# Softmax over 16,384 rows on one core: row tiles of 15 in place of tiles of up to 25

## The chip, the cores and the metric

The kernel runs on one core of a Trainium2 chip. The metric is the time of one execution on the device, in microseconds. The time before is the median of four executions, 160.37 us, with a lowest of 159.57 and a highest of 161.0. A separate execution was recorded by the hardware profiler; all rows of a profile in this document come from such single executions.

## The reference

The input is a float32 array of 16 x 1024 rows of 512 elements. Every row gets a softmax with temperature 2:

```python
x_scaled = x / 2.0
x_max = np.max(x_scaled, axis=-1, keepdims=True)
exp_x = np.exp(x_scaled - x_max)
return exp_x / np.sum(exp_x, axis=-1, keepdims=True)
```

The data is 33.55 MB in and 33.55 MB out, and there is no reuse between rows.

## The kernel before

**Tiles.** The 16,384 rows are 128 partitions x 128 rows. A tile of r rows takes 128 x r consecutive rows of the input and puts r of them on each partition, so that each partition's piece is one contiguous run of r x 2 KB, both in the input and on the chip. `TILES` (line 10) lists the tiles as (rows, place in the arena). There are 8 of them, called tile 0 to tile 7 here: 3, 5, 15, 25, 25, 25, 20 and 10 rows. The arena (`ARENA`, line 13) holds 98 rows, and everything is computed in place in it. The first six tiles fill it exactly; tiles 6 and 7 begin again at its start, over tiles that have been stored.

**Loads.** Each tile is loaded by one DMA. SP issues load 0 and ACT all others. Loads 0 and 1 are put ahead of the entry barrier (`early`, lines 152 to 154); load 1 is cut into three DMAs (`SPREAD`, line 114). Loads 2 to 5 follow at once (`loads`, lines 156 to 158). Loads 6 and 7 are the late ones (`LATE`, line 12): ACT waits until the stores of the tiles that they overwrite have landed (stores 0, 1, 2 for load 6, store 3 for load 7), and then issues them. `TURNS` (line 20) says where in ACT's program this happens: load 6 after the exponentials of row 72, load 7 after those of row 97.

**Exponentials.** ScalarE (ACT) takes exp(x / 2) of one row of all 128 partitions at a time, with the row's sum as a second output (line 276; line 200 for the first 3 rows). The maximum isn't subtracted; the sums are checked at the end, as told below. The rows go in chunks of `E` = 5, in the loop `exponentials` (lines 264 to 281). Before each chunk ACT takes one count of the semaphore `s_go`, which PE raises when a tile has landed (lines 189 and 190), so that PE does nothing but translate "tile landed" into "so many chunks may go" (and one small matmul at the end).

**Scaling.** VectorE (DVE) takes the reciprocals of the sums (line 165) and multiplies the rows by them (line 168). One pair of instructions serves a group of chunks of the same tile: up to 3 chunks (15 rows), or up to 2 (10 rows) for the late tiles (line 82). That makes 12 pairs.

**Stores.** SP issues one store per tile, in order, when the last group of the tile has been multiplied (`store`, lines 132 to 134, called in line 214). Last, SP waits until all stores have landed (lines 261 and 262).

**The check of the sums.** When all exponentials are done, GpSimd and VectorE count the sums that lie between 1 and 1e30, PE adds the counts over the partitions, and VectorE writes a flag (lines 175 to 186). If a sum lay outside, the loops in `rounds` would compute everything again with the maximum subtracted. With this input they run no round. VectorE, ACT and GpSimd wait there for the last store but one (`s_near`).

Of the kernel before, what the change touches and what calls it, by code (L numbers as in the profile page):

```python
# [6 lines left out]

TILES = [(3, 0), (5, 3), (15, 8), (25, 23), (25, 48), (25, 73), (20, 0), (10, 20)]  # L10

LATE = {6: (0, 1, 2), 7: (3,)}
ARENA = 98

HEAD = [3]
# [1 line left out]

SPREAD = 1

TURNS = {6: 73, 7: 98}  # L20

LO, HI = 1.0, 1.0e30
G = 64
# [3 lines left out]
def kernel(  # L27
# [16 lines left out]
    n_rows = N // P  # L44
    assert sum(r for r, _ in TILES) == n_rows

# [11 lines left out]
    tiles, base = [], 0  # L58
    for r, at in TILES:
        assert at == base % ARENA  # L60
# [11 lines left out]
    straight = sum(HEAD)  # L72
# [6 lines left out]

    pairs = []  # L80
    for k, t in enumerate(owner):
        most = 2 if t in LATE else 3
        if pairs and len(pairs[-1]) < most and owner[pairs[-1][0]] == t:
            pairs[-1].append(k)
        else:
            pairs.append([k])
    upto = [1 + max(j for j, ks in enumerate(pairs) if owner[ks[0]] == t) for t in range(len(tiles))]

    ld = [nc.alloc_semaphore(f"ld{t}") for t in range(len(tiles))]
    s_home = {t: nc.alloc_semaphore(f"s_home{t}") for t in LATE}  # L90
    s_near = nc.alloc_semaphore("s_near")
# [18 lines left out]
    def load(eng, t):  # L110
        r = tiles[t][1]
        parts = [(0, P, 0, r)]
        if t == SPREAD:
            parts = [(0, P, 0, r - 1), (0, 126, r - 1, r), (126, P, r - 1, r)]
        for p, q, lo, hi in parts:
            eng.dma_start(
                out=sb(t)[p:q, lo:hi], in_=dram(xf, t)[p:q, lo:hi]
            ).then_inc(ld[t], 16)

    stored_by = {u: s_home[t] for t, us in LATE.items() for u in us}  # L120
    for t, (_, r, at) in enumerate(tiles):
        over = {u for u, (_, ru, au) in enumerate(tiles[:t]) if at < au + ru and au < at + r}
        assert over <= {u for v, us in LATE.items() if v <= t for u in us}

    def landings(ts):
        return 16 * len(list(ts))
# [9 lines left out]
    def take(eng, sem, n):  # L136
        eng.wait_ge(sem, n).then_inc(sem, -n)  # L137
# [18 lines left out]
    def loads():  # L156
        for t in range(2, min(LATE)):
            load(nc.scalar, t)

    def program():  # L160
# [36 lines left out]
        for k, c in enumerate(HEAD):  # L197
# [4 lines left out]
                    accum_out=stats[:, b : b + 1],  # L202
                )
            ins.then_inc(s_exp, 1)
        done = straight
        for t, us in LATE.items():
            exponentials(done, TURNS[t])
            nc.scalar.wait_ge(s_home[t], landings(us))
            load(nc.scalar, t)
            done = TURNS[t]  # L210
        exponentials(done, n_rows)

        for t in range(len(tiles)):
            store(nc.sync, t)
# [49 lines left out]
    def exponentials(first, end):  # L264
        row = nc.scalar.alloc_register(f"row{first}")
        nc.scalar.reg_mov(row, first)
        with nc.scalar.While(lambda: nc.scalar.snap(row, min_val=first, max_val=end) < end):  # L267
            now = nc.scalar.snap(row, min_val=first, max_val=end - E)
            take(nc.scalar, s_go, 1)
            at = nc.s_assert_within(  # L270
                now % ARENA, 0, ARENA - E,
                skip_runtime_bounds_check_because="no chunk reaches over the arena's end",
            )
            for r in range(E):
                data = arena[:, r : ARENA - E + 1 + r][:, bass.ds(at, 1)]
                ins = nc.scalar.activation(  # L276
                    out=data, in_=data, func=Exp, scale=0.5,
                    accum_out=stats[:, r : n_rows - E + 1 + r][:, bass.ds(now, 1)],
                )
            ins.then_inc(s_exp, 1)  # L280
            nc.scalar.reg_add(row, row, E)
# [12 lines left out]
    nc.switch_body(here, parent=None, valid_engines=[i.engine for i in jumps])  # L294
    loads()
    program()


# [28 lines left out]
```

## Time and profile before

| what | value |
|---|---|
| median of 4 executions | 160.37 us (159.57 to 161.0) |
| the profiled execution, as a whole | 161.27 us |
| its span, from the first to the last event of the program | 159.9 us |
| exponentials, ACT line 276 | 125 x 615 ns, and 125 reads of the sum x 188 ns |
| multiply of 15 rows, DVE line 168 | 4 x 8157 ns |
| multiply of 10 rows | 6 x 5492 ns |
| multiply of 5 rows / of 3 rows | 2824 ns / 1758 ns, once each |
| loads of 6400 KB (25 rows), issue to landing | 52.4 us (median of 3) |
| load of 3840 KB (15 rows) | 15.0 us |
| stores of 6400 KB, issue to landing | 42.3 us (median of 3) |
| last load, 2560 KB: issued at 101.06 us | 31.2 us to landing |
| last store, 2560 KB: issued at 144.65 us | 15.2 us to landing |

The span is the time of the core from the program's first event to its last; what lies around it (1.37 us in this execution) isn't in the profile. "ACTq" and "SPq" in the rows are the instruction queues of ACT and SP: what an engine waits for there is a semaphore that such a queue instruction tests. "DMA" in the table of slices is the mean busy share of the core's 16 DMA engines in 40 equal slices of the span, in tenths. The TensorE clock granted was 1.0 throughout.

The stores are issued by SP at 10.0, 14.6, 35.7, 58.8, 79.6, 106.2, 128.3 and 144.65 us, and the late loads by ACT at 73.05 and 101.06 us.

### The profile page before, as it was taken

Reading aid. Unit: us, or ns where it says so; the run is one execution under the profiler, and the core shown is the slowest. Engines: PE = TensorE matmul, PEld = TensorE weight load, DVE = VectorE, ACT = ScalarE, POOL = GpSimd, SP = SyncE. Lnnn points to the kernel's source line nnn. Section 1 sums busy time; section 2 is a strip of 40 time slices with the busy share of each in tenths; the row PEclk is TensorE's granted clock in tenths of the full one; section 3 lists DMA queues with packets and bytes.
Section 4 is the critical chain, followed back from the end, with each engine's and each line's share of the span. In section 5 each row is a group of like instructions: output and inputs, shape, how many; then the busy total and the mean of one; then the engine's idle time right before and its main releaser. Section 6 shows DMA issues by size and latency. Waiting matters only on the chain. (4 is left out here: it accounts for less than half of the span.)

```text
span 159.9 us, 656 instructions
## 1 busy us (share of the span) xinstructions
PE 0.2 (0%) x2; PEld 0.1 (0%) x2; DVE 72.9 (46%) x27; ACT 80.5 (50%) x257; POOL 0.9 (1%) x6
## 2 busy tenths in 40 slices
PE   0000000000000000000000000000000000000000
PEld 0000000000000000000000000000000000000000
DVE  0056001990089960699900099950088900292000
ACT  0870598019996099990029995004996008700000
POOL 0000000000000000000000000000000000100000
DMA  7999999899989897999988999999898999898993
GB/s 266 389 484 416 484 459 436 374 402 492 479 320 446 361 520 343 448 456 538 410 384 379 537 405 407 471 394 466 374 487 364 471 492 423 387 451 369 410 441 154
DMA packets 2450, 67.12 MB, mean 420 GB/s; under 512 B 273, under 2 KB 273, under 8 KB 657
## 3 DMA queue, kind: packets, MB, share of 16 engines
q1 hardware_dynamic: 1296, 34.34, 50.1%
q10 hardware_dynamic: 1152, 32.77, 48.1%
q14 instruction: 2, 0.01, 0.0%
HBM read 33.55 MB, written 33.55 MB: 420 GB/s over the span
## 5 line engine op out<-in xcount | busy, mean ns | idle before, releaser
L276 ACT ACTIVATE arena<-arena x125 | 76.6, 615 | 53.6 <-ACTq L137 53.6
L168 DVE TENSOR_TENSOR arena<-arena,recip 128x5120 f32<-128x5120 f32 (+3 forms) x12 | 70.2, 5847 | 0.4
L165 DVE RECIPROCAL recip<-stats 128x10 f32<-128x10 f32 (+3 forms) x12 | 2.6, 220 | 71.6 <-ACT arena L276 63.6
L276 ACT ACTIVATION_READ_ACCUMULATOR arena<-arena x125 | 23.4, 188 | 0.0
L196 ACT ACT_TABLE_LOAD x1 | 1.3, 1283 | 4.6 <-issue 4.6
L200 ACT ACTIVATE arena<-arena 128x512 f32<-128x512 f32 x3 | 1.9, 618 | 0.2 <-ACTq L137 0.2
L175 POOL TENSOR_SCALAR inside<-stats 128x128 f32<-128x128 f32 x1 | 0.6, 633 | 136.2 <-ACT arena L276 136.2
L200 ACT ACTIVATION_READ_ACCUMULATOR arena<-arena 128x1 f32 x3 | 0.6, 185 | 0.0
L192 PE MATMUL total<-ones,count 128*1 128x1 f32 x2 | 0.2, 164 | 144.9 <-DVE inside L179 144.9
L179 DVE SCALAR_TENSOR_TENSOR inside<-inside,stats 128x128 f32<-128x128 f32 x1 | 0.3, 284 | 0.0
L183 DVE TENSOR_SCALAR flag<-total 1x1 int32<-1x1 f32 x1 | 0.1, 147 | 0.3 <-PE total L192 0.3
L192 PEld LDWEIGHTS total<-ones,count 128*1 128x1 f32 x2 | 0.1, 82 | 144.9 <-DVE inside L179 144.9
L174 POOL MEMSET ones<- 128x1 f32 x1 | 0.1, 98 | 2.2 <-POOLq L35 2.2
L311 POOL MEMSET const-bfloat16-1.0<- 128x1 bf16 x1 | 0.1, 101 | 0.0
L311 POOL MEMSET const-uint8-127<- 128x1 uint8 x1 | 0.1, 101 | 0.0
L311 POOL MEMSET const-float32-0.0<- 128x1 f32 x1 | 0.1, 98 | 0.2 <-issue 0.2
L311 POOL MEMSET const-float32-1.0<- 128x1 f32 x1 | 0.1, 98 | 0.0
L179 DVE DVE_READ_ACCUMULATOR inside<-inside,stats 128x1 f32 x1 | 0.1, 82 | 0.0
## 6 DMA issues: line engine op xcount, KB each, us to landing
arena<-in_x_dram ACTq DMA_DIRECT2D x3, 6400.0 KB, 52.4
out_dram<-arena SPq DMA_DIRECT2D x3, 6400.0 KB, 42.3
arena<-in_x_dram ACTq DMA_DIRECT2D x1, 5120.0 KB, 36.7
out_dram<-arena SPq DMA_DIRECT2D x1, 5120.0 KB, 25.6
arena<-in_x_dram ACTq DMA_DIRECT2D x1, 3840.0 KB, 15.0
out_dram<-arena SPq DMA_DIRECT2D x1, 3840.0 KB, 37.3
arena<-in_x_dram ACTq DMA_DIRECT2D x1, 2560.0 KB, 31.2
out_dram<-arena SPq DMA_DIRECT2D x1, 2560.0 KB, 15.2
```

Of the source, the lines that this page charges most:

```text
L165: nc.vector.reciprocal(out=recip[:, b : b + c], in_=stats[:, b : b + c])._wait_ge(s_exp, ks[-1] + 1).then_inc(s_rec, 1)
L168: nc.vector.tensor_mul(out=arena[:, a : a + c], in0=arena[:, a : a + c], in1=recip[:, b : b + c].unsqueeze(2).to_broadcast([P, c, D]),)._w ...
L174: nc.gpsimd.memset(ones[:, :], 1.0).then_inc(s_ones, 1)
L175: nc.gpsimd.tensor_scalar(out=inside[:, :], in0=stats[:, :], scalar1=LO, scalar2=HI, op0=Alu.max, op1=Alu.min,)._wait_ge(s_exp, len(sizes) ...
L179: nc.vector.scalar_tensor_tensor(out=inside[:, :], in0=inside[:, :], scalar=1.0, in1=stats[:, :], op0=Alu.mult, op1=Alu.is_equal, accum_ou ...
L183: nc.vector.tensor_scalar(out=flag[:, :], in0=total[:, :], scalar1=float(N), scalar2=float(n_rows // G), op0=Alu.is_ge, op1=Alu.mult,)._wa ...
L192: nc.tensor.matmul(total[:, :], lhsT=count[:, :], rhs=ones[:, :], start=True, stop=True)._wait_ge(s_cnt, 2).then_inc(s_tot, 1)
L196: nc.scalar.preload_act_table(Exp)
L200: ins = nc.scalar.activation(out=arena[:, b], in_=arena[:, b], func=Exp, scale=0.5, accum_out=stats[:, b : b + 1],)
L276: ins = nc.scalar.activation(out=data, in_=data, func=Exp, scale=0.5, accum_out=stats[:, r : n_rows - E + 1 + r][:, bass.ds(now, 1)],)
L311: nc = _bacc.Bacc("TRN2", target_bir_lowering=False, num_devices=1)
```

## The change

Tiles 3 to 7 become tiles 3 to 9, of 15 rows each. The places of tiles 0 to 2 stay. Six tiles of 15 rows follow the first two and end at row 98 of the arena, as before; the last two of 15 rows lie over its start, tile 8 over tiles 0, 1 and the larger part of tile 2, tile 9 over the rest of tile 2 and a part of tile 3. So loads 2 to 7 are issued at the start, and loads 8 and 9 are the late ones, with the waits that loads 6 and 7 had: stores 0, 1, 2 for load 8, store 3 for load 9.

ACT issues both late loads at one place, after the exponentials of row 82 (`TURN`), the end of tile 6. The loop of exponentials is entered twice instead of three times.

VectorE's groups are 3 chunks (15 rows) in all tiles but the last, where each chunk of 5 rows is a group of its own. With these tiles that makes 12 pairs again: 3, 5, seven times 15, and three times 5 rows.

The last store covers 15 rows instead of 10, and the last store but one (`s_near`) 15 rows instead of 20.

```diff
-TILES = [(3, 0), (5, 3), (15, 8), (25, 23), (25, 48), (25, 73), (20, 0), (10, 20)]
-
-LATE = {6: (0, 1, 2), 7: (3,)}
+TILES = [
+    (3, 0), (5, 3), (15, 8), (15, 23), (15, 38), (15, 53), (15, 68), (15, 83), (15, 0), (15, 15),
+]
+
+LATE = {8: (0, 1, 2), 9: (3,)}
...
-TURNS = {6: 73, 7: 98}
+TURN = 83
...
-        most = 2 if t in LATE else 3
+        most = 1 if t == len(tiles) - 1 else 3
...
-        done = straight
+        exponentials(straight, TURN)
         for t, us in LATE.items():
-            exponentials(done, TURNS[t])
             nc.scalar.wait_ge(s_home[t], landings(us))
             load(nc.scalar, t)
-            done = TURNS[t]
-        exponentials(done, n_rows)
+        exponentials(TURN, n_rows)
```

## The prediction

> **What bounds the kernel now.** I read the page's busy rows first, then its DMA rows, then SP's waits and the timeline of the end. In this first fence, the engines, the DMA share by slice, and the two queues (q10 carries ACT's loads, q1 SP's stores and the first load):
>
> ```profile
> span 159.9 us, 656 instructions
> PE 0.2 (0%) x2; PEld 0.1 (0%) x2; DVE 72.9 (46%) x27; ACT 80.5 (50%) x257; POOL 0.9 (1%) x6
> ...
> DMA  7999999899989897999988999999898999898993
> ...
> q1 hardware_dynamic: 1296, 34.34, 50.1%
> q10 hardware_dynamic: 1152, 32.77, 48.1%
> ...
> HBM read 33.55 MB, written 33.55 MB: 420 GB/s over the span
> ```
>
> No compute engine is busy for more than half of the span; the 16 DMA engines are busy for 98% of it. The packet records behind these rows say it more sharply: one packet is one partition's piece of a tile, every engine carries 8 packets of each full DMA, and at every whole microsecond from 2 to 157 at least 15 of the 16 engines have a packet under way. While both queues hold work an engine takes one packet of each in turn. The median packet takes 234 ns (3 rows, 6144 B), 385 (5 rows), 761 (10 rows), 1138 (15 rows), 1514 (20 rows), 1891 (25 rows), in either direction. So the time is a sum: 8 x (234 + 385 + 1138 + 3 x 1891 + 1514 + 761) = 8 x 9705 = 77.6 us for the loads of one engine, the same for its stores, 155.3 us together. Most engines end their last data packet at 157.5 us; the missing 2.2 us are the start (first packets at 1.0 to 1.8 us) and stretched packets. Two engines end late, at 159.0 and 159.5, and the slower one lands at 159.9: it sets the span.
>
> Next, who waits for whom (line waited for: us, times, longest), and the end of the timeline (start, duration, engine, line):
>
> ```profile
> ACT arena L276 <- ACTq L137: 53.6, 7, 11.9
> ```
> ```profile
> SPq L134 <- DVE arena L168: 139.6, 8, 26.2
> SPq L262 <- DMA out_dram<-arena: 14.9, 1, 14.9
> ```
> ```profile
> 138.89 0.21 DVE L165 RECIPROCAL recip<-stats 128x10 f32<-128x10 f32 x1 [10.65 <-ACT arena L276]
> ...
> 139.13 5.49 DVE L168 TENSOR_TENSOR arena<-arena,recip 128x5120 f32<-128x5120 f32 x1
> ...
> 144.65 0.33 SPq L134 DMA_DIRECT2D out_dram<-arena  x1
> ```
>
> ACT waits for loads, and SP for VectorE, but neither wait holds the end. The last store is issued at 144.65, while the store before it has packets on the engines until 151.7 on most (153.5 on the slowest): the issue came 7 to 9 us ahead of its turn. The last 14.9 us are only queued stores draining. Two questions decide the change: does it alter the sum of packets, and does a queue ever run dry.
>
> **The change, part by part.** *Packets.* After: 8 x (234 + 385 + 8 x 1138) = 8 x 9723 = 77.8 us each way, 155.6 together: +0.29 us. Two more loads and two more stores also write 4 more completions per engine, 9 ns each: +0.04. The start of a DMA on the engines is the unknown: three starts in the trace stretch the packets beside them by some 0.35, 0.15 and 0.3 us (at 6.4, 13.9 and 45.6 us), the other fifteen or so show nothing on all engines. Four more starts thus cost 0 to 1.4 us; I take 0.1. Sum: +0.4 us.
>
> A rule speaks against the change here. The Trainium skill, page "DMA: Bandwidth & Descriptors", section "Anatomy of one DMA", gives each DMA a fixed cost of some 2.0 us beside its bytes (fitted for DMAs that GpSimd issues). Four more DMAs would be +8 us, 168.4. The row against it: the third load's first packet starts at 16.78, while the second's last one is ending (16.94), with no gap. With a later DMA already queued the fixed part is hidden, so I use the rows; the rule is worth its 2 us only where a queue is empty.
>
> *Issue.* ACT issues six 15-row loads up front instead of four loads. The four took 0.36, 0.46, 0.48 and 0.50 us, so two more are about 1.1 us, and the first exponential goes from 6.03 to about 7.1, the first store from 10.0 to 11.1. Loads queued until beyond 80 us cover that; without them it would be 1.1 us. ACT's two late loads (0.34 each) now both stand at row 83, where ACT would be waiting anyway. SP's two more issues (0.33 each) fall in its 139.6 us of waiting.
>
> *VectorE.* 12 multiplies before and after. Before, 33.0 + 32.6 + 2.8 + 1.8 = 70.2 us; after, 1.76 + 2.82 + 7 x 8.16 + 3 x 2.82 = 70.2. Per 15-row tile 9.2 us of exponentials and 8.4 of VectorE lie inside a period of 8 x 2 x 1.138 = 18.2 us. Zero, hidden by DMA.
>
> *Turns.* I walk the two queues with these durations, in us on a typical engine. The first store's packets began 3.64 after its issue (13.64), so now at 14.7. Beside 15-row loads it takes 8 x (0.234 + 1.138) = 11.0, to 25.7, the second 8 x (0.385 + 1.138) = 12.2, to 37.9. Taking the 2.2 lost us as lost by then, the loads have done 37.9 - 2.2 - 5.0 = 30.7 of their 77.8. Thereafter the turns are equal, 18.2 for each tile: loads 4 to 9 end at 41.1, 59.3, 77.5, 95.7, 113.9, 132.1; stores 2 to 6 end at 56.1, 74.3, 92.5, 110.7, 128.9; then store 7 alone from 132.1 to 139.6, store 8 to 148.7, store 9 to 157.8.
>
> *Waits.* Load 8 is issued when tile 6 is through ACT: 77.5 + 0.6 + 9.3 = 87.4, up to 1.9 later for a lagging engine. It needs stores 0 to 2 (56), and load 9 needs store 3 (74): both long home. Behind these waits on ACT stand only the exponentials of tile 7, whose load ends at 95.7; so the wait on store 3 costs nothing unless it slips by more than 13 us, and load 8 enters its queue 6 to 8 us before load 7 has drained (before: 7.1 and 6.4 us). A store is issued 18.4 after its load has ended (0.6 landing and wait, 9.3 ACT, 0.3 + 8.16 VectorE): stores 3 to 8 come 5 to 15 us ahead of their turns.
>
> *The end.* After the last load's last packet: 0.33 to land and 0.34 to the first exponential (131.95, 132.28, 132.62 in the trace), then 15 rows to the last reciprocal 9.32 (17.93 to 27.25 in the trace, against 6.27 for 10 rows), then reciprocal and 5-row multiply 3.05 (against 5.73) and 0.03: 13.1 us, against 12.7. With 1.9 us for a lagging engine store 9 is issued at 132.1 + 1.9 + 13.1 = 147.1. Its turn is at 148.7 on a typical engine and 150.6 on the lagging one, which sets the end: 3.5 us ahead. How long does an issue take to its first packet? 1.02 on an idle queue (the first load), 2.15 on ACT's, 3.64 behind busy packets (the first store). So 0 is what I book, with -0 and +0.1 at the trace's ends for the lagging engine; the others may idle half a us and still end before it. Where 8.8 us of cover stood, 3.5 are left.
>
> Against the profiled execution: 159.9 + 0.4 = 160.3 of span. That execution as a whole took 161.27, 1.37 more than its span and 0.9 more than the median of 160.37, so I put the 0.4 on the median: **160.8 us**.
>
> **Rivals.** *The stores run dry at the end (slower).* The last load needs all 16 engines, and turns can slip: the first store landed at 29.63 on its slowest engine, 28.14 on the next, a turn lost. If the last load loses one turn on the slowest engine it ends 1.14 later, and that engine's stores are 1.14 further: the cover falls by 2.3 to 1.2 us, against 1.0 to 3.6 needed, so 0 to 2.4 us are lost; two turns lose 2.1 to 4.7. It decides from a cover under about 2 us, and gives 161.8 to 164. For it: this is the thinnest cover in the ledger. Against: any time in which loads run alone (a late first store, a gap before store 2) brings the last load forward and adds cover.
>
> *The lag goes (faster).* The two late engines lost their time in single stretched packets of 25 rows (0.92 us at 45.6; 0.40, 0.30, 0.31 and 0.62 between 114 and 121). If that hangs on the big packets or on unequal turns, the span falls by 1.6 (third-latest engine) to 2.05: 160.8 - 1.6 = 159.2 to 158.7. Against: the other 25-row packets ran at 1891.
>
> *Each DMA pays its fixed cost:* 168.4, against the rows above.
>
> *The change does nothing that can be measured:* this is the likeliest case itself.
>
> **How the numbers follow.** Sum as worked out: 0.63, 159.6 to 161.8 (the four runs of before spread over 1.4 us). Dry at the end: 0.18. Lag goes: 0.16. Fixed cost or a thing unseen: 0.03. About 1%, that is 158.8 and 162.0, is what a measurement of this kernel can tell from no change. Faster by more needs the whole lag: 0.11. Slower by more: most of the dry case, the unseen one, and four costly starts: 0.20. Within: 0.69. The range takes the milder half of both rivals: 158.9 to 162.6.
>
> **What would show it.** Right: DMA slices as full as before, packets of 1138 ns, bytes the same, VectorE at 70 us in 12 multiplies, the first store issued near 11, late loads near 88, the last store issued at 145 to 147.5, SP's last wait shrunk from 14.9 to about 13. Dry end: packets of the last store beginning after a gap behind the one before. Wrong in kind: packets longer than 1138 ns for equal bytes, or a load queue that is empty near 96 us.

## The result, and the profile after

The changed kernel takes 159.88 us (median of 42 executions), the kernel before 160.34 (63 executions, among them the four of the first table). The ratio is 0.9973, with a 95% interval of 0.996 to 0.9986. That is a gain of 0.4 us, clear of its interval, where a loss of 0.4 us was forecast. It is smaller than the 1% that was named as the limit of what a measurement can tell; with this many executions the limit is finer. Seven of the 42 executions took 170.95 to 173.36 us and are left out of the ratio; of e3 and e14 below, which have the same middle tiles, 11 of 44 took 166.87 to 172.75 us, and no execution of before or of a version with other middle tiles took over 164.6; counted in, they make the mean of the 42 161.9 us against 160.4 before, and what causes them is open, since none was profiled.

The page of the changed kernel, busy rows and DMA rows, as they were read before:

```profile
span 158.5 us, 659 instructions
PE 0.2 (0%) x2; PEld 0.1 (0%) x2; DVE 73.2 (46%) x27; ACT 80.6 (51%) x257; POOL 0.9 (1%) x6
...
DMA  6999998989898999999999999999989898989895
...
q1 hardware_dynamic: 1584, 34.34, 50.5%
q10 hardware_dynamic: 1440, 32.77, 48.5%
...
HBM read 33.55 MB, written 33.55 MB: 423 GB/s over the span
```

The reader sees the same balance: no compute engine above 51%, the DMA engines at 99%, the same bytes. VectorE's multiplies by shape (busy time, mean ns):

```profile
L170 DVE TENSOR_TENSOR arena<-arena,recip 128x7680 f32<-128x7680 f32 x7 | 57.1, 8158 | 0.2
...
L170 DVE TENSOR_TENSOR arena<-arena,recip 128x2560 f32<-128x2560 f32 x4 | 11.3, 2825 | 0.1
...
L170 DVE TENSOR_TENSOR arena<-arena,recip 128x1536 f32<-128x1536 f32 x1 | 1.8, 1758 | 0.0
```

They sum to 70.2 us, as before. What SP waited for, and the timeline of the end:

```profile
SPq L136 <- DVE arena L170: 139.2, 10, 20.1
SPq L262 <- DMA out_dram<-arena: 13.1, 1, 13.1
```
```profile
141.92 0.19 DVE L167 RECIPROCAL recip<-stats 128x5 f32<-128x5 f32 x1
...
142.15 2.83 DVE L170 TENSOR_TENSOR arena<-arena,recip 128x2560 f32<-128x2560 f32 x1
...
145.00 0.33 SPq L136 DMA_DIRECT2D out_dram<-arena  x1
```

The last store is issued at 145.0, and by the packet records its first packets follow directly on those of the store before it, at 148.3 to 148.8: 3.3 to 3.8 us of cover. So the tail is as the ledger had it. What has gone, against the first profile, is the lateness of two engines. The 16 engines each report their landing of the last store; per profile, the median landing and by how much the last two were behind it:

```
profile                    span    median   last but one   last
before (161.27 us)         159.9   157.9    +1.5           +2.0
after (159.82 us)          158.5   157.9    +0.4           +0.5
```

The typical engine ends at the same moment in both. The whole 1.4 us between these two spans is the two late engines.

They aren't there in every execution of before. Its executions lie in two groups: of the 62 compared, 33 from 159.57 to 160.35 (median 159.80) and 29 from 160.56 to 161.26 (median 160.84). The changed kernel has one group, 35 executions from 159.77 to 160.08 (median 159.87). So the gain is made of two terms: the upper group gone, which is worth 29/62 x 1.04 = 0.49 us in the mean, less 0.07 us that the changed kernel is slower than the lower group.

### The profile page after: what moved, and what is told of

It reads as the page before. It is cut to its first block, busy times and chain, and to the rows that moved or that the text cites. A ratio compares the mean times of both kernels' runs of the same rounds, so it can differ in the third digit from the quotient of the medians.

```text
span 158.5 us, 659 instructions
## 1 busy us (share of the span) xinstructions
PE 0.2 (0%) x2; PEld 0.1 (0%) x2; DVE 73.2 (46%) x27; ACT 80.6 (51%) x257; POOL 0.9 (1%) x6
## 5 line engine op out<-in xcount | busy, mean ns | idle before, releaser
L170 DVE TENSOR_TENSOR arena<-arena,recip 128x7680 f32<-128x7680 f32 (+2 forms) x12 | 70.2, 5847 | 0.4
L167 DVE RECIPROCAL recip<-stats 128x15 f32<-128x15 f32 (+2 forms) x12 | 2.7, 224 | 71.7 <-ACT arena L276 62.8
```

The source lines that it names most:

```text
L167: nc.vector.reciprocal(out=recip[:, b : b + c], in_=stats[:, b : b + c])._wait_ge(s_exp, ks[-1] + 1).then_inc(s_rec, 1)
L170: nc.vector.tensor_mul(out=arena[:, a : a + c], in0=arena[:, a : a + c], in1=recip[:, b : b + c].unsqueeze(2).to_broadcast([P, c, D]),)._w ...
```

## The experiments

The question was which part of the change keeps the engines together. "Upper" below counts executions from 160.4 us on, and each batch of experiments ran with the kernel before beside it: 22 of 43 (e1 to e4), 22 of 58 (e5 to e8), 27 of 59 (e9 to e11) and 29 of 59 (e12 to e14) upper.

**Are the two groups the late engines?** e1 and e7 are the kernel before, unchanged, each with a profile.

> The kernel before, unchanged, once more with a profile. Its executions fall in two groups, near 159.8 and near 160.8 us. All theories: if this execution is of the lower group, the spread of the last store's 16 landings (2.2 us in the first profile, of the upper group) is under 0.8 us and no data packet after 50 us is stretched by more than 0.25 us; if it is of the upper group, two engines end 1.5 to 2 us late again. Chance alone (nothing in the tiles makes an engine late) has no view on which.

> The kernel before, unchanged, for a profile of an execution of its lower group (near 159.8 us); a second of the upper group would add nothing. In the lower group both theories expect the stretched packets between 100 and 125 us to be missing and the 16 last landings within 0.8 us.

Both fell in the upper group (160.96 and 161.23). In e1 one engine is late and not two (last +1.7 us, last but one +0.5). The lower group was caught by e8, which differs only in VectorE's last groups:

```diff
-        most = 2 if t in LATE else 3
+        most = 1 if t == len(tiles) - 1 else 3
```

> Before, with the last tile (10 rows) scaled by 5 rows: the VectorE part of the change alone. The last store is issued 2.7 us earlier, at 142.0 instead of 144.65, but its turn comes at 151.5 anyway: no effect, both groups as before, median ratio 1.000 within 0.003.

e8: 159.87, ratio 1.0011 (0.9987 to 1.0035), 9 of 20 upper; the VectorE part alone does nothing to before, as expected. Its profiled execution took 159.68. The last two microseconds, in windows of e7 (first fence) and e8 (second); the last two columns are the mean busy share of the DMA engines and GB/s:

```profile
156.00:158.00 2.00, 0.00 (x0) 0.00 (x0) 0.00 (x0) 0.00 (x0) 0.00 (x0) 1.00 0.72 307
158.00:160.00 2.00, 0.00 (x0) 0.00 (x0) 0.00 (x0) 0.00 (x0) 0.00 (x0) 1.00 0.05 20
```
```profile
156.00:158.00 2.00, 0.00 (x0) 0.00 (x0) 0.00 (x0) 0.00 (x0) 0.00 (x0) 1.00 0.50 215
158.00:160.00 2.00, 0.00 (x0) 0.00 (x0) 0.00 (x0) 0.00 (x0) 0.00 (x0) 1.00 0.00 0
```

After 158 us e7 still moves data on a few engines, e8 on none. The next table says how far the last engine was behind the median, at four landings. Its last column is the stretch of store 4's packets (25 rows): what the packets begun between 106 and 122 us took beyond their median of 1.89 us, summed over those with more than 60 ns too much. (In after, store 4 has 15 rows and runs from 75 to 93 us.)

```
profile   took     store 0   store 2   store 4   last store   store 4 stretched by
before    161.27   +1.8      +2.5      +2.3      +2.0         1.6 us, 4 packets
e1        160.96   +1.8      +2.3      +2.5      +1.7         1.0 us, 4 packets
e7        161.23   +1.8      +2.4      +2.7      +1.9         2.1 us, 8 packets
e8        159.68   +0.3      +0.3      +0.6      +0.5         none
after     159.82   +0.3      +0.3      +0.3      +0.5         none
```

In the three upper profiles one or two engines lose a turn at the first store, with 25-row load packets in the other queue, and the same profiles show stretched packets of store 4. Either could be what counts. The stretch of store 4 is not the whole lateness: in the first profile the two engines ended 3.7 us behind a typical one, taken together, of which 1.6 us is store 4's packets and some 1.8 us load packets that were stretched more than those of the other engines (0.9 us in the longest, at 45.6 us); in e7 2.1 and some 1.2 of 3.4. Nor does a late engine need the slip: in the first profile one engine had slipped at the first store and two ended late, the second falling behind during store 4 (last but one +0.6 at store 3, +2.0 at store 4).

**Middle tiles or late tiles?** e2 gives before the late tiles of after, e3 gives after the late tiles of before.

```diff
-TILES = [(3, 0), (5, 3), (15, 8), (25, 23), (25, 48), (25, 73), (20, 0), (10, 20)]
+TILES = [(3, 0), (5, 3), (15, 8), (25, 23), (25, 48), (25, 73), (15, 0), (15, 15)]
```
```diff
-    (3, 0), (5, 3), (15, 8), (15, 23), (15, 38), (15, 53), (15, 68), (15, 83), (15, 0), (15, 15),
+    (3, 0), (5, 3), (15, 8), (15, 23), (15, 38), (15, 53), (15, 68), (15, 83), (20, 0), (10, 20),
```

> The middle tiles of before (25 rows), the late tiles of after (15 and 15 rows), the last tile scaled by 5 rows. Packet sum 155.3 us per engine, as before. Theory of unequal turns (an engine is made late where its two queues alternate packets of different sizes): 25 beside 15 until 130 us, so late engines stay: median 160.0 to 160.9, executions in two groups, landings of the last store spread over more than 1 us in the upper one. Theory of big packets (25 rows in themselves are stretched): the same, 160.0 to 160.9. Theory of the late tiles (the 10- and 20-row tiles at the end make engines late): one group at 159.6 to 159.9.

> The middle tiles of after (15 rows), the late tiles of before (20 and 10 rows), the last tile scaled by 5 rows. Packet sum 155.6 us per engine, as after. Theory of unequal turns: 20 and 10 beside 15 from 96 to 132 us, so late engines come back: median 160.0 to 160.9 or two groups. Theory of big packets: no packet above 20 rows, so one group at 159.8 to 160.0 as after. Theory of the late tiles: late engines come back, as for unequal turns.

e2: 160.81, 12 of 20 compared executions upper, ratio 1.0009 (0.9986 to 1.0033). Its profiled execution (162.21) shows no slip at the first store (+0.3) and one engine that fell 3.1 us behind during store 4. e3: its compared executions run from 159.73 to 160.03, none upper, ratio 0.9977 (0.9956 to 0.9998). The 25-row middle tiles carry the upper group; the late tiles don't. Unequal turns as such are rejected by e3, which has 20 and 10 rows beside 15.

**What is the cover at the end worth?** e4 is after with the last tile scaled 15 rows at once.

```diff
-        most = 1 if t == len(tiles) - 1 else 3
+        most = 3
```

> After, but the last tile is scaled 15 rows at once instead of by 5. The last store is issued 5.3 us later, at 150.4 instead of 145.0. My ledger: store 8 ends at 148.6 on a typical engine, so the engines run dry; with 1.0 us from issue to first packet the loss is 2.8 us (162.7 us), with 2.15 us 3.9 us (163.8). If the cover at the end were worth nothing (the last packets come from elsewhere), 159.9 as after.

162.45 us (four executions, 162.32 to 162.52); ratio to before 1.0139 (1.0086 to 1.0192), 2.57 us above after. Its timeline:

```profile
142.21 8.16 DVE L170 TENSOR_TENSOR arena<-arena,recip 128x7680 f32<-128x7680 f32 x1
...
150.39 0.33 SPq L136 DMA_DIRECT2D out_dram<-arena  x1
```

The engines end store 8 at 148.3 to 148.8 and begin store 9 at 151.2 to 151.4. So an issue on an empty queue takes 0.8 to 1.0 us to its first packet, and the engines stood still for 2.4 to 3.1 us. The groups of 5 rows are therefore a part that the 15-row last tile needs: without them the change would have been a loss of 2 us. On the tiles of before they bring nothing (e8).

**Packet size or addresses?** e5 has equal turns of 20 rows, e6 leaves the tiles of before where they are and cuts the DMAs.

```diff
-TILES = [(3, 0), (5, 3), (15, 8), (25, 23), (25, 48), (25, 73), (20, 0), (10, 20)]
+TILES = [(3, 0), (5, 3), (20, 8), (20, 28), (20, 48), (20, 68), (20, 0), (20, 20)]
...
-ARENA = 98
+ARENA = 88
...
-TURNS = {6: 73, 7: 98}
+TURNS = {6: 68, 7: 88}
...
-        most = 2 if t in LATE else 3
+        most = 1 if t == len(tiles) - 1 else 3
```
```diff
         if t == SPREAD:
             parts = [(0, P, 0, r - 1), (0, 126, r - 1, r), (126, P, r - 1, r)]
+        elif r == 25:
+            parts = [(0, P, 0, 15), (0, P, 15, 25)]
...
-        eng.dma_start(out=dram(of, t), in_=sb(t)).then_inc(sem_of.get(t, s_end), 16)
+        r = tiles[t][1]
+        for lo, hi in [(0, 15), (15, 25)] if r == 25 else [(0, r)]:
+            eng.dma_start(
+                out=dram(of, t)[:, lo:hi], in_=sb(t)[:, lo:hi]
+            ).then_inc(sem_of.get(t, s_end), 16)
```

(Here and in e11 to e13 the counts that the waits test are changed to match, which the cuts of the code leave out.)

> Tiles of 3, 5 and six times 20 rows (arena of 88 rows, late loads after rows 68 and 88, last tile scaled by 5 rows): equal turns of 40960-byte packets throughout. Packet sum 155.3 us per engine, 0.3 below after; by my ledger the last store is issued 3.5 us ahead of its turn. Theory of packet size (an engine is made late by packets above some size): if 20 rows are above it, two groups at 159.7 and 160.8 as before; if below, one group at 159.5 to 159.8. Theory of the 25-row layout (the addresses of 25-row tiles): one group at 159.5 to 159.8. If every version without 25-row tiles but with fewer packets is at or under after: below 159.9.

> Before, but each 25-row tile is loaded and stored by two DMAs, rows 0 to 14 and rows 15 to 24 of every partition: the same tiles, addresses, groups and issue places, with packets of 30720 and 20480 bytes in place of 51200. Packet sum 8 x 2 x 3 x 8 ns = 0.4 us more than before. Theory of packet size: one group at 160.0 to 160.2, no data packet after 50 us stretched by more than 0.25 us, last landings spread under 0.8 us. Theory of the layout: two groups, near 160.1 and 161.2, with two late engines in the upper one.

e6: 160.22, ratio 1.0007 (0.9989 to 1.0024), one group from 160.07 to 160.47 (three of its 21 lie just over the 160.4), last landings within 0.7 us of the median. That is the lower group plus the 0.4 us that its packets were expected to cost more; the same addresses in smaller packets have no second group. The layout is rejected, packet size stands. e5 fits neither expectation: 160.16, 21 of 22 spread from 159.77 to 160.51 and one at 160.97, ratio 1.0007 (0.9991 to 1.0024). At 20 rows there are no two groups, and no narrow one either.

**Early or later, loads or stores?** e9 puts 15-row tiles first and 25-row tiles later, e10 only one 25-row tile, beside the first stores; e11 cuts the stores of e6 alone and leaves the loads whole.

```diff
-TILES = [(3, 0), (5, 3), (15, 8), (25, 23), (25, 48), (25, 73), (20, 0), (10, 20)]
+TILES = [
+    (3, 0), (5, 3), (15, 8), (15, 23), (25, 38), (25, 63), (10, 88), (20, 0), (10, 20),
+]
```
```diff
-TILES = [(3, 0), (5, 3), (15, 8), (25, 23), (25, 48), (25, 73), (20, 0), (10, 20)]
+TILES = [
+    (3, 0), (5, 3), (15, 8), (25, 23), (15, 48), (15, 63), (20, 78), (15, 0), (15, 15),
+]
...
-        most = 2 if t in LATE else 3
+        most = 1 if t == len(tiles) - 1 else 3
```

(The late loads are tiles 7 and 8 in both, issued after 63 and 88 rows in e9, after 78 and 98 in e10.)

> Tiles 3, 5, 15, 15, 25, 25, 10, then late 20 and 10: the first stores (3 and 5 rows) go out beside 15-row loads, the 25-row packets come later. Packet sum 155.4 us. In the upper-group profiles of before one or two engines lose a turn at the first store (its landing there is 1.8 us behind the median) and stay behind to the end; in the lower-group one none does. Theory of the slip at the start (the turn is lost beside 25-row loads at the first stores, and what it costs is fixed there): one group at 159.7 to 160.0, all landings within 0.8 us. Theory of the big packets later (engines fall behind wherever 25-row packets run, as two of them did after 100 us): two groups, near 159.8 and 160.9.

> The reverse: tiles 3, 5, 15, 25, 15, 15, 20, then late 15 and 15: only the load beside the first stores has 25 rows. Packet sum 155.4 us. Slip at the start: two groups, 159.8 and 160.5 to 160.9, with a store landing 1.8 us late on one or two engines from the first store on. Big packets later: one group at 159.7 to 160.0; a slip at the first store, where there is one, is made good later.

> Before, with the stores of the 25-row tiles cut into two DMAs (rows 0 to 14, 15 to 24), the loads whole. Packet sum 155.5 us, +0.2. Slip at the start (it is made of load packets): two groups, 160.0 and 161.0. Store packets (the packets stretched at 112 to 121 us in the upper group are 25-row stores): one group at 159.9 to 160.1.

e9: 161.04, ratio 1.004 (1.0017 to 1.0064), from 160.23 to 162.18: worse than before, so 15 rows beside the first store don't help while 25-row stores follow. It isn't a clean test of the slip: in its profile store 1 still met 25-row loads, from 28.3 us on, and six engines lost their turn there (+2.3 to +2.5). e10: 160.11, 3 of 22 upper, ratio 0.999 (0.9972 to 1.0009). Its profile shows the early slip (+1.8) and an end at +1.0: a slip is partly made good. e11: 159.84, all 22 executions from 159.62 to 160.05, ratio 0.9968 (0.9951 to 0.9986). With whole 25-row loads and cut stores the upper group is gone: it needs the packets of the 25-row stores. (The reverse, loads cut and stores whole, wasn't run.) It also answers the slip: e11 is before, instruction for instruction and packet for packet, until store 3 begins at 72 us, so its engines have the same chances to lose a turn at the first store. A slip alone doesn't make an execution slow. The profile of e6 shows it directly: two engines were 2.0 us behind at the first store, the last one was 0.6 behind at store 2 and 0.6 at the end.

**Which store?** e12 cuts store 4 alone, e13 stores 3 and 5, e14 is after once more beside them.

```diff
+CUT = {4}
...
-        eng.dma_start(out=dram(of, t), in_=sb(t)).then_inc(sem_of.get(t, s_end), 16)
+        r = tiles[t][1]
+        for lo, hi in [(0, 15), (15, 25)] if t in CUT else [(0, r)]:
+            eng.dma_start(
+                out=dram(of, t)[:, lo:hi], in_=sb(t)[:, lo:hi]
+            ).then_inc(sem_of.get(t, s_end), 16)
```
```diff
-CUT = {4}
+CUT = {3, 5}
```

> Before, with only store 4 (25 rows, the one under way from 100 to 122 us, when the last load starts, and the one with the packets stretched at 112 to 121 us) cut into rows 0 to 14 and 15 to 24. Packet sum 155.4 us. If engines fall behind where store 4's 25-row packets stand beside the 10-row last load: one group at 159.6 to 159.9, which would be at or under after. If it is any 25-row store: two groups as before, 159.8 and 160.9.

> The complement: stores 3 and 5 cut, store 4 whole. If store 4 beside the last load is the place: two groups, 159.9 and 160.9. If any 25-row store does it in proportion: upper group in fewer executions than before, or a smaller step. If store 3 or 5 is the place: one group at 159.8 to 160.0.

> After, unchanged, on the same chip as the two others: one group at 159.8 to 160.0, the yardstick for whether a whole-tile version with one cut store beats it.

e12: 159.83, 22 of 22 from 159.70 to 160.19, ratio 0.9979 (0.9961 to 0.9996). e14: its compared executions from 159.81 to 160.09, ratio 0.9964 (0.9946 to 0.9983). e13: 159.96, 6 of 22 upper, 0.9993 (0.9969 to 1.0016). So one cut store takes all of the upper group, and cutting the two others leaves some of it. Whether those two help at all isn't settled by 6 of 22 against 29 of 59. In e13's profile an engine lost a turn at the first store, was 2.8 us behind at store 1, and was level again (+0.6) when the cut store 3 had landed; whether it was the cut that let it catch up, this one profile can't say. The cut is seen in e12's page among the DMA issues (count, KB each, us to landing):

```profile
out_dram<-arena SPq DMA_DIRECT2D x2, 6400.0 KB, 37.4
out_dram<-arena SPq DMA_DIRECT2D x2, 3840.0 KB, 36.1
...
out_dram<-arena SPq DMA_DIRECT2D x2, 2560.0 KB, 34.9
...
arena<-in_x_dram ACTq DMA_DIRECT2D x1, 2560.0 KB, 22.0
```

Two stores of 6400 KB are left of three; a piece of 3840 and one of 2560 KB have joined stores 2 and 7, which had these sizes before. The last row is the last load: 22.0 us to its landing, where before it took 31.2. So the cut changes more than the packets of one store: load packets get through sooner beside smaller ones, and all loads have ended at 120.9 us, where they end at 130.3 to 132.0 in the profiles of before and of e8. In after and e3, which have no upper group either, they end at 131.8 and 132.0, so the earlier end isn't needed; whether it helps in e11 (121.5) and e12, beside the size of the packets, no run tells. (The earlier last store that follows from it isn't the reason: e8 had an earlier one too, and as many executions in the upper group as before.) e11 and e12 reach the time of the changed kernel by a cut of one to three stores, with tiles, loads and VectorE as before; the intervals overlap, so neither is shown to beat it. What stretches the packets of one engine wasn't found.

## Why the prediction was wrong

*Bound, packets, VectorE: right.* The DMA rows carry the time, 15-row packets took 1138 ns, and 13 of the 16 engines ended at 157.3 to 157.6 where 157.8 was booked. The term was too large, though: the 0.4 us for more packets and starts came out as 0.07 over the lower group of before. Where the rest went is open.

*Issue, turns, waits: right in their consequence.* The first store was issued at 10.89 (11.1 booked) and began at 14.8 (14.7). The landings of stores 2 to 5, 56.8, 75.0, 93.2 and 111.3, stand 0.6 to 0.7 behind the packet ends of the ledger. The exponentials of tile 6 ended at 87.2 (87.4 booked), but the late loads were issued at 84.0 and 84.4 already, five exponentials ahead:

```profile
84.03 0.33 ACTq L118 DMA_DIRECT2D arena<-in_x_dram  x1
...
84.40 0.74 ACTq L118 DMA_DIRECT2D arena<-in_x_dram  x1
...
86.53 0.61 ACT L276 ACTIVATE arena<-arena  x1
87.05 0.19 ACT L276 ACTIVATION_READ_ACCUMULATOR arena<-arena  x1
```

This only added cover.

*The end: right.* 145.0 for the last store (145 to 147.5), and no dry queue. The price of a dry one was near as well: e4 lost 2.57 us, and first packets came 0.8 to 1.0 us after the issue, where 1.0 to 3.6 was the range.

*The rule of 2 us per DMA:* four more DMAs cost nothing of the kind, in this change or in e6 (six more, 0.4 us). Where a queue did run empty, in e4, the last store took 0.8 to 1.0 us from its issue to its first packets and some 0.4 from its last packets to its landing, 1.2 to 1.4 us beside its bytes and not 2.

*The step that failed* is the one that "put the 0.4 on the median". It carried the two late engines, seen in one profile of before, over into the changed kernel, and set against the rival "The lag goes" that "the other 25-row packets ran at 1891". That the others are unharmed says nothing on the stretched ones: two engines out of 16 are enough to set the end. About half of what they lost they lost in store packets of 25 rows, which the change removes, and with those gone the upper group is gone. The rival, given 0.16 and 159.2 to 158.7 us, named the big packets as one of two possible causes; e11 and e12 show that it hangs on those of the stores, and e3 rejects the other, unequal turns. It overstated its worth, because it took the profiled execution (161.27, of the upper group) for the typical one: in the mean of before the late engines are worth 0.49 us, not 1.6 to 2.05. So of the 0.8 us between the forecast (+0.4) and the result (-0.4), 0.49 is this step and 0.33 the size of the packet term. The four times of before showed the two groups, 161.0, 159.57, 160.86, 159.88: two pairs, which the prediction read as a spread of 1.4 us.

## What to carry to other kernels

Where a kernel is bound by DMA and every byte and packet is accounted for, look at the landings of the single engines: a span is set by the last of 16, and one profile may show an execution in which one of them is late. Times in two groups say that there is such a thing to be removed. Here it was enough to cut one large store in two, and 15-row tiles did the same; a 15-row last tile needs its multiply cut as well, or the store queue runs dry.

## What the runs showed of the hardware that wasn't expected

- Store packets of 51200 bytes that alternate with load packets can be stretched, by 0.1 to 0.7 us each, while the others run at 1.89 us: on one or two engines in the profiles of before, on six at once in e9. The same stores in packets of 30720 and 20480 bytes weren't, by more than 0.11 us, in the profiles of e6 and e11. Load packets were stretched too, by up to 0.9 us on one engine (before, at 45.6 us).
- An engine can lose a turn between its two queues when a small store starts beside large loads (a landing 1.8 us behind the median at the first store). It can be made good later (e6, e13).
- A DMA issued on an empty store queue at the end of the program had its first packets 0.8 to 1.0 us later (e4); the first store, issued with loads under way, had them 3.6 us (before) and 3.9 us (after) later.
- ACT's queue issued a load 3.2 us before the exponentials ahead of it in the program had run (84.0 against 87.2 us).
